# A four-sublayer hybrid trunk in split float32: the order of its first microseconds, and its first projection item in blocks of 128 tokens

## The chip, the core and the metric

The kernel runs on one core of one Trainium2 chip, as one launch. The metric is the device time in microseconds (us), median of three runs. Engines are called as in the profile: PE is the matrix engine (PEld its weight loads), DVE the vector engine, ACT the scalar engine, POOL the GpSimd engine, SP the engine that only issues loads and stores.

## The reference

The input `x` is one sequence of 512 tokens with 1024 features, in float32. It passes two layers. Each has a token mixer and a gated feed-forward block with a short causal convolution, and after each of these four sublayers stands `x = LayerNorm(alpha * x + f(x))`. Layer 0 mixes by gated linear attention, layer 1 by a gated delta rule. The change lies in the very first step, the input projection of layer 0:

```python
def gla_mixer(x, w_in, w_gk2, b_gk, norm_w, w_out):
    proj = x @ w_in                      # (512 x 1024) @ (1024 x 3088)
    q, k, v, gate, gk_lr = jnp.split(proj, [hk, 2 * hk, 2 * hk + hv, 2 * hk + 2 * hv], axis=-1)
    gk = jax.nn.log_sigmoid((gk_lr @ w_gk2 + b_gk).astype(jnp.float32)) / GLA_NORMALIZER
    ...
```

`gk_lr` has 16 columns and `w_gk2` is the 16 x 512 low-rank factor of the decay.

## The kernel before

All activations are kept feature-major: `xh` and `xl` hold x transposed, as 8 chunks of 128 features by 512 tokens. Every float32 operand of a large product is split in two: a high part, rounded to the PE's type fp32r, and a low part, the rest (`split_out`: ACT writes the high part, DVE subtracts it from the source). A product is three products: high by high, low x by high weight, high x by low weight. `wh`/`wl` are the two parts of a weight, `raw` the weight as loaded (three buffers), `wts` holds four split weights.

An **item** is 128 output columns of a projection: a 1024 x 128 weight, 8 chunks, 24 products into one PSUM bank (`fm_mms`). The plan is a list of items; `prefetch` issues the loads and splits of the next items (`issue`), and `fm_items` runs them. The first four items (`HEADSTART`: a query head, a key head, the low-rank item, a query head) run in two halves of 256 tokens, since the tokens come in four blocks of 128: the first half of all four needs blocks 0 and 1 alone. `late` (true for the first half of the first item) puts the eight low-weight products last. The low-rank item (`issue_rep`, the "rep" item) has 16 columns, repeated to 96.

The opening (`load_x`) runs so: `h` tiles (one for a block of 128 tokens and half the features) are loaded, block 0 from the SP queue, block 1 from the ACT queue; `x_part` transposes one `h` tile on PE in four steps into a bank `xT` and splits it into `xh`, `xl`. Two constant products on the tile `reset` into a bank `warm` stand ahead of the transposes, two behind them. The weight of the first item is loaded in two halves on the SP queue behind block 0 of x, and split behind all four x parts. Blocks 2 and 3 are loaded after it, and split by the task `second`, which is run (`pump`) between products.

The order of work on an engine is the order of the program, kept by hand where it matters (`keep_in_program_order` on PE while `pin` is set; `behind`, and `opening`, which puts the splits of the first items behind the first x parts). Later tasks are set by a clock of planned costs (`clk`, `spawn`, `until`). `gla_consts` loads the low-rank factor `gk` six times over, one for each group of 16 rows, from the POOL queue, and splits it as `gk2`; its first use is the product `z` of `prepare`.

Of the kernel before, what the change touches and what calls it, by code (L numbers as in the profile page):

```python
# [15 lines left out]
P = 128  # L16
# [36 lines left out]
class Trunk:  # L53
# [3 lines left out]
    def __init__(self, ctx, tc):  # L57
        self.tc = tc
        self.nc = nc = tc.nc
        self.n = 0  # L60
        ec = ctx.enter_context
        ap = ec(tc.tile_pool(name="acts", bufs=1))
        self.xh = ap.tile([P, NC, S], F32R, name="xh", tag="xh")
        self.xl = ap.tile([P, NC, S], F32R, name="xl", tag="xl")
        self.wp = ec(tc.tile_pool(name="wts", bufs=WB))
        self.mp = ec(tc.tile_pool(name="mem", bufs=SLOTS))
        self.rp = ec(tc.tile_pool(name="raws", bufs=RAWB))
        self.cp = ec(tc.tile_pool(name="const", bufs=1))
# [10 lines left out]
        nc.gpsimd.memset(self.reset, 1.0)  # L79
        nc.gpsimd.memset(c4(self.reset)[:, :, 0:1], 0.0)  # L80
# [12 lines left out]
        self.tabled = None  # L93
        self.wide = None
        self.block = None
        self.next_block = 0.0
        self.late = []
        self.first = None


    def uid(self, s):
# [118 lines left out]
    def issue(self, item):  # L220

        nc = self.nc
        if item[0] == "rep":
            return self.issue_rep(*item[1:])
        raw = self.rp.tile([P, 1024], F32, name=self.uid("raw"), tag="raw")
        used = 1024
        if item[0] == "fm":
            _, w, col = item
            r3 = raw.rearrange("p (c f) -> p c f", c=NC)
            w3 = w[:, col:col + P].rearrange("(c p) f -> p c f", p=P)  # L230
            step = NC if self.issued else NC // 2
# [66 lines left out]
    def fm_mms(self, ps, w, lo, hi, late=False):  # L298

        o = ps[:, lo:hi]  # L300
        if not isinstance(w, list):
            for c in range(NC):
                for i, x in enumerate((self.xh, self.xl)):
                    self.mm(ps[:96, lo:hi], w[:, c, :96], x[:, c, lo:hi], c + i == 0, c + i == NC)
                if c % 2:
                    self.pump()
            return
        if late:
            for c in range(2 * NC):
                wt = w[c % NC // 4][c // NC][:, blk(c % 4)]  # L310
                self.mm(o, wt, self.xh[:, c % NC, lo:hi], c == 0, c == 2 * NC - 1)
                if c < NC:
                    self.mm(o, wt, self.xl[:, c, lo:hi], False, False)
                if c % 2:
                    self.pump()
            return
        for c in range(NC):
            xh, xl = self.xh[:, c, lo:hi], self.xl[:, c, lo:hi]
            wh, wl = (t[:, blk(c % 4)] for t in w[c // 4])
            self.mm(o, wh, xh, c == 0, False)  # L320
            self.mm(o, wh, xl, False, False)
            self.mm(o, wl, xh, False, c == NC - 1)
            if c % 2:
                self.pump()

    def fm_items(self, items):
# [112 lines left out]

    def opening(self, *parts):  # L440

        if self.issued < 4:
            for ins, other in zip(parts, self.first):
                self.behind(ins, other)

    def rsqrt(self, y, x, n):

# [35 lines left out]
    def load_x(self, x):  # L483
# [1 line left out]
        nc = self.nc  # L485
        self.h = [[self.slot("h") for _ in range(2)] for _ in range(NTB)]

        def load(eng, tb):
            for hf in range(2):
                eng.dma_start(self.h[tb][hf], x[blk(tb), blk(hf, S)])  # L490
                self.set(("h", tb, hf))

        def constant(n):
            for _ in range(n):
                self.tc.keep_in_program_order(nc.tensor.matmul(ps, self.ident, self.reset, start=True, stop=True))  # L495
# [12 lines left out]
        self.look = LOOKAHEAD  # L508
        self.prefetch()
        for tb in range(2, NTB):  # L510
            load(nc.sync, tb)

        def second():
            for tb in range(2, NTB):
                for hf in range(2):
                    self.x_part(tb, hf)
                yield 1.2

            for t, row in self.late:
# [229 lines left out]
    def gla_consts(self, w_gk2, b_gk, norm_w):  # L749
        nc = self.nc  # L750

        raw = self.slot("gk")
        for i in range(6):
            nc.gpsimd.dma_start(raw[16 * i:16 * i + 16, :], w_gk2)
        self.gk2 = self.keep([96, S], "gk2", F32R)
        nc.scalar.copy(self.gk2, raw[:96, :])
        nc.vector.tensor_sub(self.gk2[32:64, :], raw[32:64, :], self.gk2[32:64, :])
        self.gla_nw = self.keep([P, 256], "gla_nw")
        self.late.append((self.gla_nw, norm_w))

# [665 lines left out]
```

## Time and profile before

| | |
|---|---|
| median of 3 runs | 1278.29 us (1278.29 to 1278.38) |
| the profiled execution's own time | 1277.96 us |
| its span | 1276.2 us |
| PE busy | 1263.8 us, 99% of the span |
| DVE, ACT, POOL busy | 783.5, 552.8, 111.1 us |
| moved by DMA | 126.53 MB, mean 99 GB/s |

The span runs from the first to the last instruction of the profiled execution; what lies around it is 1.8 us. A row of a timeline has the start, the duration, the engine, the line and the operation, what it writes and reads, how often, and in brackets how long its engine had been idle and who ended that. The durations of products are modelled to the end of their pipeline, so two products that follow each other overlap; the time that a product costs is the distance between two starts. A product of two fp32 operands makes two rows, a product of fp32r operands one row. Shapes are partitions by elements; the profile writes both types as f32 on PE.

### The profile page before, as it was taken

What the parts mean: (1) busy time and instruction counts of PE and PEld (TensorE: products, weight loads), DVE (VectorE), ACT (ScalarE), POOL (GpSimd) and SP (SyncE); (2) the same over time, 40 slices, a digit from 0 to 9 for tenths busy, and PEclk for the clock granted to TensorE, in tenths of its full rate; (3) what the DMA queues carried; (4) which work ended last, traced back from release to release, by engine and by line L of the source; (5) the groups of instructions that cost most, each with busy time, mean ns of one, the idle gap of its engine ahead of it and who ended that gap; (6) DMA issues with size and microseconds to landing.
All of it is one profiled execution on the core that took longest, in us unless ns stands there. A gap on an engine that the chain in (4) does not pass through costs nothing.

```text
span 1276.2 us, 17247 instructions
## 1 busy us (share of the span) xinstructions
PE 1263.8 (99%) x6686; PEld 1070.0 (84%) x6686; DVE 783.5 (61%) x1381; ACT 552.8 (43%) x1050; POOL 111.1 (9%) x153
## 2 busy tenths in 40 slices
PE   9999999999999999999999999999999999999997
PEld 8878888988888888889888888988988888888886
DVE  3953466676643466555789955679577653366656
ACT  4654444634421344435765544543644431244430
POOL 4000000070000000001013120100052000000000
PEclk9999999999999999999999999999999999999999
DMA  7322224143333333351354331234053333333331
GB/s 200 116 69 66 67 85 131 50 129 103 99 99 97 93 93 98 100 151 66 101 150 114 119 77 51 68 116 134 16 151 104 93 98 99 99 99 99 94 104 66
DMA packets 167234, 126.53 MB, mean 99 GB/s; under 512 B 16104, under 2 KB 139818, under 8 KB 167152
## 3 DMA queue, kind: packets, MB, share of 16 engines
q1 hardware_dynamic: 162832, 116.28, 30.7%
q0 software_dynamic: 3888, 8.50, 2.2%
q8 instruction: 52, 0.85, 0.3%
q10 hardware_dynamic: 432, 0.66, 0.2%
q14 instruction: 30, 0.25, 0.1%
HBM read 119.63 MB, written 5.78 MB: 98 GB/s over the span
## 4 chain that ended last, share of the span: by engine, by line
PE 94%; DVE 3%; ACT 1%; issue 1%; DMA 0%; POOL 0%; DVEq 0%; ACTq 0%; POOLq 0%
PE fm L160 50%; PE tm L160 35%; PE o L160 2%; PE xT L177 1%; PE R L160 1%; PE V L160 1%; PE qkT L177 1%; PE vn L160 1%; PE pq L160 1%; PE pg L160 1%; PE yT L177 1%; DVE wl L438 1%; PE s L160 0%; PE warm L495 0%; PE qs L160 0%
## 5 line engine op out<-in xcount | busy, mean ns | idle before, releaser
L438 DVE TENSOR_TENSOR wl<-raw,wh 128x1024 fp32r<-128x1024 f32 (+1 forms) x190 | 238.7, 1258 | 314.0 <-ACT wh L438 313.8
L160 PE MATMUL fm<-xh,wh 128*128 128x512 f32 (+2 forms) x1104 | 404.3, 367 | 0.0
L160 PE MATMUL fm<-xl,wh 128*128 128x512 f32 (+2 forms) x1104 | 401.5, 365 | 0.0
L160 PE MATMUL fm<-xh,wl 128*128 128x512 f32 (+1 forms) x1088 | 397.0, 366 | 0.0
L438 ACT CAST wh<-raw 128x1024 fp32r<-128x1024 f32 (+1 forms) x190 | 198.9, 1047 | 276.6 <-PE tm L160 166.3
L160 PEld LDWEIGHTS fm<-xh,wh 128*128 128x128 f32 (+1 forms) x1104 | 207.8, 188 | 33.1 <-ACT wh L438 0.4
L160 PEld LDWEIGHTS fm<-xl,wh 128*128 128x128 f32 (+1 forms) x1104 | 207.9, 188 | 32.4
L160 PEld LDWEIGHTS fm<-xh,wl 128*128 128x128 f32 x1088 | 204.7, 189 | 33.7 <-DVE wl L438 0.2
L681 DVE SCALAR_TENSOR_TENSOR conv<-fm,ffn_cw,conv 128x511 f32<-128x511 f32 (+1 forms) x176 | 130.7, 746 | 3.0
L160 PE MATMUL tm<-wl,gh 128*128 128x512 f32 x290 | 112.4, 388 | 0.0
L160 PE MATMUL tm<-wh,gl 128*128 128x512 f32 x290 | 112.4, 388 | 0.0
L160 PE MATMUL tm<-wh,gh 128*128 128x512 f32 x290 | 112.4, 388 | 0.0
L438 ACT CAST gh<-conv 128x512 fp32r<-128x512 f32 x44 | 27.3, 621 | 125.1 <-DVE conv L696 124.9
L160 PE MATMUL tm<-wh,xh 128*128 128x512 f32 x192 | 79.6, 415 | 0.1
L160 PE MATMUL tm<-wh,xl 128*128 128x512 f32 x192 | 75.2, 392 | 0.0
L160 PE MATMUL tm<-wl,xh 128*128 128x512 f32 x192 | 75.1, 391 | 0.0
L691 ACT ACTIVATE conv<-conv 128x512 f32<-128x512 f32 x44 | 27.8, 632 | 95.1 <-DVE conv L681 95.0
L160 PEld LDWEIGHTS tm<-wh,gl 128*128 128x128 f32 x290 | 54.5, 188 | 11.2
L160 PEld LDWEIGHTS tm<-wl,gh 128*128 128x128 f32 x290 | 54.5, 188 | 11.2
L160 PEld LDWEIGHTS tm<-wh,gh 128*128 128x128 f32 x290 | 54.5, 188 | 11.1
L679 ACT ACTIVATE conv<-fm,ffn_cw 128x512 f32<-128x512 f32 x88 | 60.0, 681 | 0.2
L982 DVE SCALAR_TENSOR_TENSOR conv<-fm,gdn_cw,conv 128x509 f32<-128x509 f32 (+2 forms) x72 | 53.3, 744 | 4.1 <-ACT conv L980 3.5
(279 smaller groups left out, 1536.0 us busy)
## 6 DMA issues: line engine op xcount, KB each, us to landing
raw<-in_ffn_w_in_dram SPq DMA_DIRECT2D x88, 512.0 KB, 3.7
raw<-in_ffn_w_out_dram SPq DMA_DIRECT2D x44, 512.0 KB, 3.7
raw<-in_gdn_w_in_dram SPq DMA_DIRECT2D x32, 512.0 KB, 4.1
raw<-in_gla_w_in_dram SPq DMA_DIRECT2D x23, 512.0 KB, 3.5
raw<-in_gla_w_out_dram SPq DMA_DIRECT2D x8, 512.0 KB, 3.6
raw<-in_gdn_w_out_dram SPq DMA_DIRECT2D x8, 512.0 KB, 3.7
hd<-h POOLq DMA_DIRECT2D x8, 256.0 KB, 2.5
dt<-drow POOLq DMA_DIRECT2D x8, 256.0 KB, 5.1
```

Source lines behind the costliest of these rows:

```text
L160: t = self.nc.tensor.matmul(out, a, b, start=start, stop=stop)
L177: t = self.nc.tensor.transpose(out, a, self.ident[:n, :n])
L438: return self.nc.scalar.copy(dst_h, src), self.nc.vector.tensor_sub(dst_l, src, dst_h)
L679: nc.scalar.activation(a, ps, AF.Identity, scale=tap(2))
L681: nc.vector.scalar_tensor_tensor(a[:, d:], ps[:, :S - d], tap(2 - d), a[:, d:], ALU.mult, ALU.add)
L691: nc.scalar.activation(a, a, AF.Gelu)
L982: self.conv = nc.vector.scalar_tensor_tensor(a[:, d:], ps[:, :S - d], tap(3 - d), a[:, d:], ALU.mult, ALU.add)
```

## The change

Seven edits, all in the opening:

1. The tile `reset` is set by DVE, not by POOL, and the constant products use it alone; the second pair of them is gone.
2. All four `h` tiles of blocks 0 and 1 are loaded from the SP queue. The two halves of the first weight go to the ACT queue, ahead of everything on it. The loads of the second and third item follow block 1 on the SP queue, then blocks 2 and 3.
3. The splits are chained in the order in which they are needed: x part (0,0), first half of the first weight, x part (0,1), second half.
4. The first item runs by `first_mms`: block 0 with 24 products of 128 tokens, then the transposes of block 1 (`between`), then block 1 with 24 products of 128 tokens.
5. The second item has its low-weight products last (`late`, now for item 1).
6. The low-rank factor is loaded by a task (`factor`): a POOL copy that reads the last x low part of block 1 stands ahead of the six loads, and the split of `gk2` is put behind the last x part.
7. In `opening`, each split is put behind the one before it, rather than all behind the last x part.

```diff
-        nc.gpsimd.memset(self.reset, 1.0)
-        nc.gpsimd.memset(c4(self.reset)[:, :, 0:1], 0.0)
+        nc.vector.memset(self.reset, 1.0)
+        nc.vector.memset(c4(self.reset)[:, :, 0:1], 0.0)
...
-                nc.sync.dma_start(r3[:, c:c + step, :], w3[:, c:c + step, :])
+                (nc.sync if self.issued else nc.scalar).dma_start(r3[:, c:c + step, :], w3[:, c:c + step, :])
...
-        for n in (S, used) if self.issued == 0 else (used,):
-            cols = slice(0 if n < used or self.issued else S, n)
-            self.opening(*self.split_out(wh[:, cols], wl[:, cols], raw[:, cols]))
+        pieces = [blk(j, S) for j in range(used // S)] if self.issued == 0 else [slice(0, used)]
...
+    def first_mms(self, ps, w):
+
+        def terms(tb, i):
+            for x in (self.xh, self.xl):
+                for c in range(4 * i, 4 * i + 4):
+                    self.mm(ps[:, blk(tb)], w[i][0][:, blk(c % 4)], x[:, c, blk(tb)], c == 0 and x is self.xh, False)
+
+        def low(tb, i):
+            for c in range(4 * i, 4 * i + 4):
+                self.mm(ps[:, blk(tb)], w[i][1][:, blk(c % 4)], self.xh[:, c, blk(tb)], False, c == NC - 1)
+
+        for tb in range(2):
+            for i in range(2):
+                terms(tb, i)
+                low(tb, i)
+            if tb == 0:
+                self.between()
+        self.pump()
...
-                self.fm_mms(banks[i], ws[i], half * 256, half * 256 + 256, self.pin and not half and i == 0)
+                if self.between and not half and i == 0:
+                    self.first_mms(banks[i], ws[i])
+                    self.between = None
+                else:
+                    self.fm_mms(banks[i], ws[i], half * 256, half * 256 + 256, self.pin and not half and i == 1)
...
-        load(nc.sync, 0)
-        load(nc.scalar, 1)
+        for tb in range(2):
+            for hf in range(2):
+                load(tb, hf)
+        self.prefetch()
...
-        constant(2)
-        for hf in range(2):
-            for tb in range(2):
-                self.first = self.x_part(tb, hf)
-        constant(2)
+        self.opening(*self.x_part(0, 0))
+        self.opening(*self.pieces[0]())
+        self.opening(*self.x_part(0, 1))
+        self.opening(*self.pieces[1]())
...
+        def factor():
+            raw = self.slot("gk")
+
+            nc.gpsimd.tensor_copy(raw[:, :1], self.xl[:, NC - 1, 255:256].bitcast(F32))
+            for i in range(6):
+                nc.gpsimd.dma_start(raw[16 * i:16 * i + 16, :], w_gk2)
+            yield 8.0
+            yield from self.until(("x", NTB - 1))
+            self.behind(nc.scalar.copy(self.gk2, raw[:96, :]), self.last[0])
+            self.behind(nc.vector.tensor_sub(self.gk2[32:64, :], raw[32:64, :], self.gk2[32:64, :]), self.last[1])
```

What PE runs first, before the change (`xT_112`, `xT_126` are the two halves of block 0, `xT_119`, `xT_133` those of block 1; `fm_198` is the bank of the first item; behind the rows shown come fourteen more of its products by `wh_145`):

```order
L495 MATMUL warm_109<-reset_88,ident_80 128x512 x2
L177 MATMUL xT_112<-ident_80,h_96 128x128 x4
L177 MATMUL xT_119<-ident_80,h_98 128x128 x4
L177 MATMUL xT_126<-ident_80,h_97 128x128 x4
L177 MATMUL xT_133<-ident_80,h_99 128x128 x4
L495 MATMUL warm_109<-reset_88,ident_80 128x512 x2
L160 MATMUL fm_198<-xh,wh_145 128x256
L160 MATMUL fm_198<-xl,wh_145 128x256
```

And after it, as far as the first products of the second item (`xT_117`, `xT_126` block 0; `xT_183`, `xT_190` block 1; `fm_158` the first item, `fm_250` the second):

```order
L536 MATMUL warm_114<-reset_88 128x512 x2
L178 MATMUL xT_117<-ident_80,h_96 128x128 x4
L178 MATMUL xT_126<-ident_80,h_97 128x128 x4
L161 MATMUL fm_158<-xh,wh_111 128x128 x4
L161 MATMUL fm_158<-xl,wh_111 128x128 x4
L161 MATMUL fm_158<-xh,wl_112 128x128 x4
...
L178 MATMUL xT_183<-ident_80,h_98 128x128 x4
L178 MATMUL xT_190<-ident_80,h_99 128x128 x4
L161 MATMUL fm_158<-xh,wh_111 128x128 x4
...
L161 MATMUL fm_250<-xh,wh_199 128x256
```

The 24 products of 256 tokens have become 48 of 128, and the transposes of block 1 stand between the two sets.

ACT before, at the same place (`wh_145` first item, `wh_153` second):

```order
L490 DMA h_98<-in_x_dram 128x512
L490 DMA h_99<-in_x_dram 128x512
...
L438 CAST xh<-xT_112 128x4x128
L438 CAST xh<-xT_119 128x4x128
L438 CAST xh<-xT_126 128x4x128
L438 CAST xh<-xT_133 128x4x128
L438 CAST wh_145<-raw_142 128x512 x2
L438 CAST wh_153<-raw_151 128x1024
```

ACT after (`wh_111` first item, `wh_199` second):

```order
L234 DMA raw_108<-in_gla_w_in_dram 128x4x128 x2
...
L469 CAST xh<-xT_117 128x4x128
L469 CAST wh_111<-raw_108 128x512
L469 CAST xh<-xT_126 128x4x128
L469 CAST wh_111<-raw_108 128x512
L469 CAST xh<-xT_183 128x4x128
L469 CAST xh<-xT_190 128x4x128
L469 CAST wh_199<-raw_197 128x1024
```

The two halves of the weight are split among the x parts of block 0, and block 1 comes after them; DVE's subtractions follow in the same order.

More of the change, by code (lines that the diff above doesn't have):

```diff
@@ L258, in issue @@
         wl = self.wp.tile([P, 1024], F32R, name=self.uid("wl"), tag="wl")
-        for n in (S, used) if self.issued == 0 else (used,):
-            cols = slice(0 if n < used or self.issued else S, n)
-            self.opening(*self.split_out(wh[:, cols], wl[:, cols], raw[:, cols]))
+        pieces = [blk(j, S) for j in range(used // S)] if self.issued == 0 else [slice(0, used)]
+        split = lambda cols: self.split_out(wh[:, cols], wl[:, cols], raw[:, cols])
+        if self.issued == 0:
+            self.pieces = [lambda cols=cols: split(cols) for cols in pieces]
+        elif self.issued < 4:
+            self.opening(*split(pieces[0]))
+        else:
+            split(pieces[0])
         self.vec(1.24)
@@ L308, in fm_mms @@
         if late:
[L309 to L313, printed above, removed]
+            for c in range(NC):
+                for x in (self.xh, self.xl):
+                    self.mm(o, w[c // 4][0][:, blk(c % 4)], x[:, c, lo:hi], c == 0 and x is self.xh, False)
                 if c % 2:
+                    self.pump()
+            for c in range(NC):
+                self.mm(o, w[c // 4][1][:, blk(c % 4)], self.xh[:, c, lo:hi], False, c == NC - 1)
+                if c % 4 == 3:
                     self.pump()
@@ L324, in fm_mms @@
                 self.pump()
+    def first_mms(self, ps, w):
+        def terms(tb, i):
+            for x in (self.xh, self.xl):
+                for c in range(4 * i, 4 * i + 4):
[9 more added lines that the diff above has]
+                self.between()
+        self.pump()
     def fm_items(self, items):
@@ L336, in fm_items @@
                     banks.append(self.psum("fm"))
-                self.fm_mms(banks[i], ws[i], half * 256, half * 256 + 256, self.pin and not half and i == 0)
+                if self.between and not half and i == 0:
+                    self.first_mms(banks[i], ws[i])
+                    self.between = None
+                else:
+                    self.fm_mms(banks[i], ws[i], half * 256, half * 256 + 256, self.pin and not half and i == 1)
                 if half:
@@ L440, in opening @@
     def opening(self, *parts):
-        if self.issued < 4:
+        if self.first is not None:
             for ins, other in zip(parts, self.first):
                 self.behind(ins, other)
+        self.first = parts
     def rsqrt(self, y, x, n):
@@ L486, in load_x, with load, between @@
         self.h = [[self.slot("h") for _ in range(2)] for _ in range(NTB)]
-        def load(eng, tb):
+        def load(tb, hf):
+            nc.sync.dma_start(self.h[tb][hf], x[blk(tb), blk(hf, S)])
+            self.set(("h", tb, hf))
+        for tb in range(2):
             for hf in range(2):
[L490 to L495, printed above, removed]
-        load(nc.sync, 0)
-        load(nc.scalar, 1)
+                load(tb, hf)
+        self.prefetch()
+        self.look = 0
         self.tc.keep_in_program_order(nc.scalar.copy(self.warm, self.one))
         ps = self.psum("warm")
-        constant(2)
-        for hf in range(2):
-            for tb in range(2):
-                self.first = self.x_part(tb, hf)
-        constant(2)
[L508 to L511, printed above, removed]
+        for _ in range(2):
+            self.tc.keep_in_program_order(
+                nc.tensor.matmul(ps, self.reset[:, :P], self.reset, start=True, stop=True))
+        self.opening(*self.x_part(0, 0))
+        self.opening(*self.pieces[0]())
+        self.opening(*self.x_part(0, 1))
+        self.opening(*self.pieces[1]())
+        self.set(("x", 1))
+        def between():
+            for hf in range(2):
+                self.opening(*self.x_part(1, hf))
+            self.look = 1
+            self.prefetch()
+            for tb in range(2, NTB):
+                for hf in range(2):
+                    load(tb, hf)
+            self.look = LOOKAHEAD
+        self.between = between
         def second():
@@ L515, in second @@
                 for hf in range(2):
-                    self.x_part(tb, hf)
+                    self.last = self.x_part(tb, hf)
                 yield 1.2
@@ L750, in gla_consts @@
         nc = self.nc
-        raw = self.slot("gk")
-        for i in range(6):
-            nc.gpsimd.dma_start(raw[16 * i:16 * i + 16, :], w_gk2)
         self.gk2 = self.keep([96, S], "gk2", F32R)
-        nc.scalar.copy(self.gk2, raw[:96, :])
-        nc.vector.tensor_sub(self.gk2[32:64, :], raw[32:64, :], self.gk2[32:64, :])
+        def factor():
[7 more added lines that the diff above has]
+            self.behind(nc.vector.tensor_sub(self.gk2[32:64, :], raw[32:64, :], self.gk2[32:64, :]), self.last[1])
+        self.spawn(factor(), 3.0)
         self.gla_nw = self.keep([P, 256], "gla_nw")
```

## The prediction

> **What bounds the kernel now.** I read the page's busy times first, then PE's waits, then the timeline of the first 14 us engine by engine, since the change moves instructions there and nearly nowhere else.
>
> ```profile
> PE 1263.8 (99%) x6686; PEld 1070.0 (84%) x6686; DVE 783.5 (61%) x1381; ACT 552.8 (43%) x1050; POOL 111.1 (9%) x153
> PE warm L495 <- POOL reset L80: 2.0, 1, 2.0
> PE xT L177 <- DVE ln_mv L557: 0.9, 1, 0.9
> PE kt L177 <- DVE sc L872: 0.8, 1, 0.8
> PE bat L177 <- DVE ba L1017: 0.4, 1, 0.4
> ```
>
> PE is busy 99% of the span, and its listed waits outside the start come to 2.1 us. So the end moves by as much as PE's stream moves. One anchor is enough: the start of the second item, at 12.97 us. From there on PE has the same products as before, in the same order but for a few steps. The rows of PE and its weight loads as far as that anchor:
>
> ```profile
> 2.00 3.78 PE L495 MATMUL warm<-reset,ident 128*128 128x512 f32 x4 [2.00 <-POOL reset L80]
> 5.58 2.98 PE L177 MATMUL xT<-ident,h 128*128 128x128 f32 x16
> 8.39 1.88 PE L495 MATMUL warm<-reset,ident 128*128 128x512 f32 x4
> 9.80 0.59 PE L160 MATMUL fm<-xh,wh 128*128 128x256 f32 x1
> ...
> 12.01 1.12 PE L160 MATMUL fm<-xh,wl 128*128 128x256 f32 x8
> 12.97 0.28 PE L160 MATMUL fm<-xh,wh 128*128 128x256 f32 x1
> 4.96 0.18 PEld L177 LDWEIGHTS xT<-ident,h 128*128 128x128 f32 x1 [0.76 <-DMA h<-in_x_dram]
> 9.79 0.19 PEld L160 LDWEIGHTS fm<-xh,wh 128*128 128x128 f32 x1 [0.35 <-ACT wh L438]
> 13.41 0.19 PEld L160 LDWEIGHTS fm<-xh,wl 128*128 128x128 f32 x1 [0.24 <-DVE wl L438]
> ```
>
> The constant products fill time only. The first h tile is there at 4.96, the transposes run from 5.58, and the first product waits for ACT's split of the weight until 9.79. From there a product of 256 tokens takes (12.97 - 12.01) / 8 = 0.12 us, the 24 of the first item about 3 us. The engines in front of it:
>
> ```profile
> 6.67 0.59 ACT L438 CAST xh<-xT 128x512 fp32r<-128x512 f32 x1 [3.45 <-PE xT L177]
> 9.11 1.15 ACT L438 CAST wh<-raw 128x512 fp32r<-128x512 f32 x2
> 7.29 0.69 DVE L438 TENSOR_TENSOR xl<-xT,xh 128x512 fp32r<-128x512 f32 x1 [7.29 <-ACT xh L438]
> 9.98 1.28 DVE L438 TENSOR_TENSOR wl<-raw,wh 128x512 fp32r<-128x512 f32 x2
> 1.01 0.53 POOL L79 MEMSET reset<- 128x512 f32 x1
> 1.84 0.11 POOL L80 MEMSET reset<- 128x4 f32 x1
> h<-in_x_dram ACTq DMA_DIRECT2D x2, 256.0 KB, 4.7
> raw<-in_gla_w_in_dram SPq DMA_DIRECT2D x2, 256.0 KB, 6.8
> 8.11 0.38 SPq L270 DMA_DIRECT2D raw<-in_gla_w_in_dram x1
> ```
>
> **Part 1: how much sooner the first product starts.** `reset` on DVE: no row shows a DVE memset, so POOL's pair is the nearest, 0.53 + 0.11, from 0.81 (when the engines' first rows start) to 1.45 instead of 2.00. It can cost between nothing and that. The constant products take 5.58 - 2.00 = 3.58 us, so the transposes start at 5.03 instead of 5.58, and not before the h tile at 4.96: -0.55, with ends 0 and -0.62. The second pair of constant products goes; it covered the wait for the weight split and costs nothing when gone. ACT's first x split comes 6.67 - 5.58 = 1.09 behind the first transpose: from 6.12 to 6.71, where before four x splits came ahead of the weight.
>
> The first weight half now leads the ACT queue, issued about 0.81. The two rows of landing bound it: 4.7 for an h tile on that queue, 6.8 for a weight half behind block 0 of x on the SP queue, so it lands between 5.5 and 7.6. (Before, the SP row at 8.11 is released by that half.) I take about 6.7, near the middle: then ACT is free just in time, and splits it to 7.34 (0.63 of the 1.15 for two). At 7.6 all that follows is 0.9 later, at 5.5 nothing changes. So the first product starts at 7.37 instead of 9.80: -2.4 us. The second half of block 0 and of the weight follow on ACT to 7.93 and 8.55, and on DVE four subtractions of 0.68 from 6.73 end at 9.5.
>
> **Part 2: what 48 narrow products cost.** No row shows an fp32r product of 128 tokens. The nearest of the same shape are products of 128 by 128 by 128 in the second mixer, those of the same type are the 0.12 above, and transposes have the same width:
>
> ```profile
> 719.21 1.95 PE L160 MATMUL pq<-conv,conv 128*128 128x128 f32 x16
> 720.91 0.48 PE L160 MATMUL fm<-xh,wh 128*128 128x512 f32 x1
> 17.89 0.91 PEld L177 LDWEIGHTS xT<-ident,h 128*128 128x128 f32 x8
> 18.01 1.03 PE L177 MATMUL xT<-ident,h 128*128 128x128 f32 x8
> 18.64 1.07 ACT L438 CAST xh<-xT 128x512 fp32r<-128x512 f32 x2 [0.98 <-PE xT L177]
> ```
>
> The 16 rows of `pq` are eight products and take 720.91 - 719.21 = 1.70 us: 0.2125 a product, 0.106 a row. A weight load of 128 columns is never closer to the next than about 0.11 (0.91 / 8 for transposes). So a narrow product costs between half of 0.12, if only its tokens count, and 0.2125, if the saving of the fp32r type is lost at this width. I take 0.2125: it is the only real product of this shape in the trace, and every fp32r product of this kernel is at least 256 wide, so nothing shows that the type keeps its rate below. A half-rate clock in the opening gives the same price by another way (rival 3).
>
> Then block 0 takes 24 x 0.2125 = 5.1, from 7.37 to 12.47; its operands are all there by 9.5, ahead of use. The transposes of block 1 (0.91 for eight) run to 13.38. They were hidden before, in the wait for the weight; now they stand on the path. ACT starts 0.63 behind the first (18.01 to 18.64) and needs 0.59: PE goes on at 13.7 instead of 13.38. Block 1 takes 5.1 more: the second item starts at 18.8. Its split, behind the x parts on ACT, ends by 15.9 and is hidden.
>
> So the anchor moves by 18.8 - 12.97 = +5.8.
>
> **Part 3: the rest.** The second item's low parts last: the wait of 0.24 at 13.41 goes, since the low weight is used 16 products later; nothing else is late there. Blocks 2 and 3 and the rep item are loaded as early as before, and their transposes come at the anchor + 3.8 or later (16 + 8 products by 0.12 and 0.115), so no new wait. The third item's raw buffer comes free with the first item's last subtraction, now 9.5 rather than 11.26.
>
> ```profile
> 1.88 3.08 POOL L754 DMA_DIRECT2D gk<-in_gla_w_gk_dram  x6
> gk<-in_gla_w_gk_dram POOLq DMA_DIRECT2D x6, 32.0 KB, 5.6
> 12.00 0.62 ACT L756 CAST gk<-gk 96x512 fp32r<-96x512 f32 x1
> 33.44 0.40 PE L160 MATMUL fm<-xh,wh 128*128 128x512 f32 x1
> 34.83 0.40 PE L160 MATMUL z<-lr,gk 96*128 96x512 f32 x1
> ```
>
> The factor: POOL's copy waits for block 1's last low part (about 15.1), then six issues of 0.51 and 5.6 to land give 23.3 at the earliest use. ACT then waits for it ahead of the fifth item's split, which PE needs at 33.44 + 5.6, and `z` at 34.83 + 5.6: 14 us of cover. Queued behind the copy on POOL are only norm weights and column rows, whose loads waited for a later x part anyway. If the cover were gone it would cost its two splits, 0.62 and about 0.68 on DVE. Six `tm` products that change places some 90 us in wait for nothing in PE's list: 0.
>
> **The sum**: +5.8 - 0.24 = +5.6. Against the profiled execution's own 1277.96 (span 1276.2, 1.8 around it) that is 1283.6; the median lies 0.33 above that execution, so **1283.9 us**.
>
> **Rivals.**
>
> *One weight load a product (0.114).* For it speaks that 0.11 is the least distance of 128-column loads and that each fp32r product is one row. Then DVE sets part of the pace: block 0 ends at 10.1, transposes 11.0, ACT's split of block 1 at 11.33, its low part at 12.04, block 1 at 14.3. Anchor +1.35, less 0.24: +1.1, or **1279.4**; 1280.3 with the weight at 7.6. The gain of 2.4 at the front is paid back by 2.5 of products and 1.2 of transposes and split.
>
> *Only the tokens count (0.06): not slower.* Then products hide behind DVE. Block 0 ends with the last subtraction, at 9.73; transposes 10.64; the low part of block 1 at 11.65; block 1 ends at 12.8: -0.17 - 0.24 = -0.4, or **1277.9**. It decides when a narrow product falls under about 0.08. For more than 0.2% the anchor would have to be at 10.6, and DVE's six subtractions of 0.69 from 6.7, with a transpose and a split between, do not end by then; so faster by 0.2% has almost no room.
> The Trainium skill, "TensorE: Matmul & The Clock Gate", section "Back-to-back issue gap", gives N / 2.4 + 2.5 ns for one product and about 81 ns in a stream with weight loads at N = 128; by 0.081 I estimate 1278.4. At N = 256 its formula gives 109 ns, where the trace has 120, and no run here shows its 128 for this type.
>
> *The clock stays low.* Before, four rows of constant products take 3.78 us at 2.00 and 1.88 at 8.39: PE starts at half rate and is at full rate after unbroken work from 2.00 to 8.39 at most. The change leaves gaps between the transposes and among the first products. If the rate rises only 5.7 us after 7.37, the first rival loses half of that: 1279.4 + 2.9 = **1282.3**; with all 48 at half rate about 1285.8. Against it: the gaps are under 1 us each.
> The same page, section "Part 1: The HAM clock gate (the "warmup" mystery)", says that about 3.4 us of activity raise the clock and an idle window of that length lowers it; by that rule, an estimate, this rival would cost at most 1.7 us, and the transposes before agree with the rise (0.91 for eight later, 2.98 for 16 early).
>
> **Chances.** Forecast 0.50, one weight load a product 0.30, only the tokens 0.08, the clock 0.12. Below 0.2% (2.6 us, about what a measurement of this kernel tells from no change) lie rival 1, most of rival 2 and a little of the clock's: slower 0.60, same 0.37, faster 0.03. The range goes from under the first rival to the forecast with a late weight (+0.9) and some of the clock: 1278.6 to 1286.0. It leaves out most of rival 2, and a forecast that also starts at half rate, together about 0.12. The forecast's own range is 1283.0 to 1285.5.
>
> **What would show it.** Right: first item's products 0.21 apart; second item at 18 to 20 us; no 0.24 wait behind it; `gk` split near 24 with no wait of PE. Wrong: products 0.11 or less apart, a first product later than 8.5 us, or a new wait of PE behind the anchor.

## The result: 1280.03 us, and the profile after

The changed kernel takes **1280.03 us** (median of 22 runs, 1279.53 to 1280.32) against 1278.27 for the kernel before in the same session (22 runs, 1277.74 to 1278.59): a ratio of **1.0014, 95% interval [1.0008, 1.0020]**, 1.76 us more. The profiled execution has 1280.23 us and a span of 1278.5, which is 2.27 us over the profiled execution of before.

First PE's waits after (engine, what waits, for what, total in us, times, longest):

```profile
PE warm L536 <- DVE reset L80: 1.7, 1, 1.7
PE xT L178 <- DVE ln_mv L599: 1.2, 1, 1.2
PE kt L178 <- DVE sc L922: 0.7, 1, 0.7
PE cols L178 <- DMA rows<-in_gdn_conv_w_dram: 0.5, 1, 0.5
PE bat L178 <- DVE ba L1067: 0.4, 1, 0.4
PE fm L161 <- ACT wh L469: 0.3, 1, 0.3
PE fm L161 <- ACT xh L469: 0.2, 1, 0.2
```

Three rows are new: the two `fm` waits of the opening, and `cols`, a wait far behind it. Now PE's timeline of the opening:

```profile
5.23 1.91 PE L178 MATMUL xT<-ident,h 128*128 128x128 f32 x8
7.48 0.73 PE L161 MATMUL fm<-xh,wh 128*128 128x128 f32 x4 [0.34 <-ACT wh L469]
8.05 0.61 PE L161 MATMUL fm<-xl,wh 128*128 128x128 f32 x4
8.49 0.61 PE L161 MATMUL fm<-xh,wl 128*128 128x128 f32 x4
...
10.28 1.06 PE L178 MATMUL xT<-ident,h 128*128 128x128 f32 x8
11.58 0.66 PE L161 MATMUL fm<-xh,wh 128*128 128x128 f32 x4 [0.24 <-ACT xh L469]
12.31 0.66 PE L161 MATMUL fm<-xl,wh 128*128 128x128 f32 x4
...
14.15 0.61 PE L161 MATMUL fm<-xh,wl 128*128 128x128 f32 x4
14.60 0.33 PE L161 MATMUL fm<-xh,wh 128*128 128x256 f32 x1
```

A row of four products starts 0.447 us behind the one before it ((8.49 - 8.05) and its like): 0.112 us a product, not 0.2125. Block 0 runs from 7.48 to 10.28, block 1 from 11.58 to 14.60, and the second item starts at 14.60, where it started at 12.97 before: +1.63. ACT, in front of it:

```profile
6.33 0.59 ACT L469 CAST xh<-xT 128x512 fp32r<-128x512 f32 x1 [2.98 <-PE xT L178]
6.81 0.62 ACT L469 CAST wh<-raw 128x512 fp32r<-128x512 f32 x1
7.33 0.59 ACT L469 CAST xh<-xT 128x512 fp32r<-128x512 f32 x1
...
10.94 1.07 ACT L469 CAST xh<-xT 128x512 fp32r<-128x512 f32 x2 [2.50 <-PE xT L178]
```

The weight's split at 6.81 follows the x split without a wait of its own, so the first weight half had landed by then.

Where the 2.27 us between the two profiled executions went: +1.63 at the second item, -0.24 for its own wait that is gone, +0.46 for `cols` at 87.46 us, and +0.33 for `ln_mv` at the second layer (1.21 against 0.88), together 2.18. The last of them is not the change's: the same changed kernel, run again, showed 1.0 there, and the kernels below show 0.6 to 1.8. The opening differs between executions too. e1 below has the same opening, and in its profile the first product starts at 6.82 and the second item at 13.87 us, since PE's eight transposes of block 0 took 1.04 us there and 1.91 here. So a few tenths between two single profiles prove little.

### The profile page after: what moved, and what is told of

The parts are those of the page before. It is cut to its first block, busy times and chain, and to the rows that moved or that the text cites. A ratio compares the mean times of both kernels' runs of the same rounds, so it can differ in the third digit from the quotient of the medians.

```text
span 1278.5 us, 17288 instructions
## 1 busy us (share of the span) xinstructions
PE 1265.1 (99%) x6706; PEld 1071.5 (84%) x6706; DVE 783.6 (61%) x1383; ACT 552.6 (43%) x1050; POOL 111.7 (9%) x152
## 4 chain that ended last, share of the span: by engine, by line
PE 91%; issue 5%; DVE 1%; DMA 1%; POOL 0%; ACT 0%; DVEq 0%; POOLq 0%; ACTq 0%
PE fm L161 48%; PE tm L161 34%; PE o L161 2%; PE xT L178 1%; PE R L161 1%; PE V L161 1%; PE qkT L178 1%; PE vn L161 1%; PE pq L161 1%; PE pg L161 1%; PE yT L178 1%; PE s L161 0%; PE qs L161 0%; PE ks L161 0%; DMA raw<-in_ffn_w_in_dram 0%
## 5 line engine op out<-in xcount | busy, mean ns | idle before, releaser
L161 PE MATMUL fm<-xh,wl 128*128 128x512 f32 (+2 forms) x1096 | 397.0, 365 | 0.0
L161 PEld LDWEIGHTS fm<-xh,wh 128*128 128x128 f32 x1112 | 208.4, 188 | 34.0 <-ACT wh L469 0.7
L161 PEld LDWEIGHTS fm<-xl,wh 128*128 128x128 f32 x1112 | 208.4, 188 | 32.5 <-DVE xl L469 0.2
```

The costliest lines, as they stand in the source:

```text
L161: t = self.nc.tensor.matmul(out, a, b, start=start, stop=stop)
```

## The experiments

Each was timed beside the kernel before, which had 1278.23 us in the runs of e1 to e4, 1278.27 in those of e5 to e8, 1278.08 in those of e9 to e12 and 1278.07 in those of e13 and e14.

### What do narrow products cost? e2, e5

e2 is the kernel before with nothing changed but the width of the first item's products:

```diff
-                self.fm_mms(banks[i], ws[i], half * 256, half * 256 + 256, self.pin and not half and i == 0)
+                if self.pin and not half and i == 0:
+                    for tb in range(2):
+                        self.fm_mms(banks[i], ws[i], tb * P, tb * P + P, True)
+                else:
+                    self.fm_mms(banks[i], ws[i], half * 256, half * 256 + 256)
```

> The kernel before with one edit: the first half of its first item runs as 48 products of 128 tokens, block by block, instead of 24 of 256. Theory A (a narrow product costs one weight load, 0.112 us): 48 x 0.112 - 24 x 0.12 = +2.5 us at the second item's start, of which 0.2 come back because the wait for the second item's low part goes: 1280.5 to 1280.8. Rival C (narrow products are only slow in the changed kernel, by its gaps; by themselves they cost half a wide one): 0, 1278.1 to 1278.3. Rival D (0.2125 a product, as predicted): +7.3, about 1285.

1280.30 us (11 runs), 2.07 over before, ratio 1.0017 [1.0008, 1.0026]. PE's timeline in e2:

```profile
8.88 0.43 PE L160 MATMUL fm<-xh,wh 128*128 128x128 f32 x1
...
10.83 1.06 PE L160 MATMUL fm<-xh,wl 128*128 128x128 f32 x8
11.72 0.28 PE L160 MATMUL fm<-xh,wh 128*128 128x128 f32 x1
...
14.40 0.33 PE L160 MATMUL fm<-xh,wh 128*128 128x256 f32 x1
```

Eight products take 11.72 - 10.83 = 0.89 us, 0.111 each. The first half of the item takes 14.40 - 8.88 = 5.52 us where 24 wide products took 12.97 - 9.80 = 3.17: 2.35 more in the traces, 2.07 in the medians. So narrowness alone makes the kernel slower by about as much as the whole change does (1.76). That 1280.30 is a little under the 1280.5 of the lower bound is not explained further; the size of the product is.

e5 goes on to 96 products of 64 tokens, to see whether 0.112 belongs to the tokens or to the product (against e2):

```diff
-                    for tb in range(2):
-                        self.fm_mms(banks[i], ws[i], tb * P, tb * P + P, True)
+                    for tb in range(4):
+                        self.fm_mms(banks[i], ws[i], tb * 64, tb * 64 + 64, True)
```

> The kernel before, with the first half of the first item as 96 products of 64 tokens instead of 24 of 256 (in the narrow kernel these were 48 of 128, 0.112 us apart, 1280.30 us). Theory A: a product costs one load of 128 weight columns, about 0.11 us, whatever its tokens: 96 x 0.112 = 10.75 us, 5.4 more than the 48 of 128, so 1285.4 to 1285.9 us. Theory C: the tokens set the distance (0.112 for 128 tokens, so 0.056 to 0.08 for 64): the 96 take 5.4 to 7.7 us, so 1280.3 to 1282.6 us.

1293.78 us (4 runs, 1293.03 to 1294.13): far over both. PE's timeline in e5 tells both parts:

```profile
9.47 0.28 PE L160 MATMUL fm<-xh,wh 128*128 128x64 f32 x1
9.58 0.28 PE L160 MATMUL fm<-xl,wh 128*128 128x64 f32 x1
...
12.93 0.36 PE L160 MATMUL fm<-xl,wh 128*128 128x64 f32 x1
13.10 0.40 PE L160 MATMUL fm<-xh,wh 128*128 128x64 f32 x1
13.32 0.40 PE L160 MATMUL fm<-xl,wh 128*128 128x64 f32 x1
```

Until 12.93 a product of 64 tokens costs 0.112 us, as one of 128 does: theory A's floor holds, and C, that tokens set the distance, is out. A floor can also be a fixed price of any product. A row of the kernel before speaks against that: 16 rows of products with 64 weight columns and 64 tokens, with the next product at 746.81 us:

```profile
745.74 1.14 PE L160 MATMUL V<-T,am 64*64 64x64 f32 x16
```

They are (746.81 - 745.74) / 16 = 0.067 us apart, and the rows of `pq`, with 128 columns, 0.106. Since 64 or 128 tokens make no difference at 128 columns, that points to the columns of the weight as the price. These products are of fp32 and fill 64 partitions, and no run varied the columns alone.

From 13.10 on a product of e5 costs 0.213 us. PE waits for nothing there; its clock fell. The stretches of e5 (from and to in us, length, PE busy and its instructions, granted clock, share of the DMA engines, GB/s):

```profile
12.00:13.00 1.00, 1.00 (x11) 0.99 1.08 348
13.00:14.00 1.00, 1.00 (x7) 0.50 1.34 223
...
28.00:32.00 4.00, 4.00 (x28) 0.74 0.00 0
```

The clock is 0.50 from 12.98 (0.02 us of the first stretch) to 30.08 (2.08 us of the last): 17.1 us. The 64-token products end at 26.33, so the fall costs 13.35 x (1 - 0.112 / 0.213) + 3.75 x (1 - 0.120 / 0.213) = 8.0 us, and theory A's 1285.4 to 1285.9 with it is 1293.4 to 1293.9, near the measured 1293.78.

### What stands between the blocks, and what would be without narrow products: e3, e4

e3 is the changed kernel with block 1 transposed and split ahead of block 0's products:

```diff
-        self.set(("x", 1))
+        for hf in range(2):
+            self.opening(*self.x_part(1, hf))
...
-            for hf in range(2):
-                self.opening(*self.x_part(1, hf))
```

> The changed kernel with the transposes and splits of block 1 ahead of the first item's products rather than between its two blocks; the later order is that of the kernel before. Theory A: the 0.87 us of transposes and the waits of 0.24 and 0.28 leave the path, but the first product now waits for the last h tile of block 1 (landed at 8.05) and its transposes: it starts at about 8.5 instead of 7.48, so the second item starts near 13.9 instead of 14.6; with the column rows' wait gone as well 1278.6 to 1278.9. Rival B (the products' width and place do not matter, the loads do): no gain at the second item, 14.6, and 1279.4.

1278.87 us (11 runs), 0.64 over before, ratio 1.0005 [0.9996, 1.0014]; theory A's numbers. In e3's timeline no transpose stands between the products of the two blocks:

```profile
8.26 0.64 PE L161 MATMUL fm<-xh,wh 128*128 128x128 f32 x4
...
10.52 0.61 PE L161 MATMUL fm<-xh,wl 128*128 128x128 f32 x4
10.96 0.61 PE L161 MATMUL fm<-xh,wh 128*128 128x128 f32 x4
...
13.64 0.33 PE L161 MATMUL fm<-xh,wh 128*128 128x256 f32 x1
```

The first product comes 0.78 later than in the changed kernel and the second item 0.96 sooner: starting block 0 ahead of block 1's transposes lost more than it gained. The `cols` wait is not in e3's list either, so some of the 1.1 us between the two kernels may be that.

e4 keeps the change's queues, `reset` and factor, but runs the first item as 24 products of 256 tokens, by halves of the features:

```diff
-        for tb in range(2):
-            for i in range(2):
-                terms(tb, i)
-                low(tb, i)
-            if tb == 0:
-                self.between()
+        for i in range(2):
+            terms(i)
+            low(i)
+            if i == 0:
+                self.between()
```

with `x_part(0, hf)`, `x_part(1, hf)` and the weight's half ahead of each other in that order.

> The changed kernel with its first item as 24 products of 256 tokens again: x parts (0,0), (1,0), first half of the weight, (0,1), (1,1), second half, and the products in the same order of need. All other edits stay. Theory A: ACT has the first half of the weight split at about 9.0 and the second at about 10.7; products as fast as before (0.12); the second item starts near 12.3, that is 0.7 sooner than before, no wait for low parts: 1277.2 to 1277.6, about 0.9 faster than the kernel before. Rival B (the loss comes from the loads' order or the low-rank factor's place): still 1279 or more.

**1277.32 us** (11 runs), 0.91 under before, ratio 0.9993 [0.9984, 1.0002]: theory A again, and the lowest median of the study, though its interval just holds 1. Its second item starts at 12.19 us, and it has no `cols` wait:

```profile
12.19 0.28 PE L161 MATMUL fm<-xh,wh 128*128 128x256 f32 x1
```

So the change's other edits, with wide products, seem good for some 0.9 us, and the narrow products, with the transposes between them and the `cols` wait, take 2.7 back (1280.03 - 1277.32). The load queues have no part in that gain: e9 below is e4 with the queues of before, and has 1277.29. What is left (`reset`, the order of the splits and products, the second item's low parts last, the later factor) no run took apart.

e8 is e4 with the `h` tiles loaded in the order of use:

```diff
-        for tb in range(2):
-            for hf in range(2):
+        for hf in range(2):
+            for tb in range(2):
                 load(tb, hf)
```

> The kernel with the first item as 24 products of 256 tokens (1277.32 us), its x tiles now loaded in the order in which they are transposed: first halves of blocks 0 and 1, then the second halves. Theory A: the wait of 0.86 us for the third tile goes, the first product starts 0.3 to 0.6 earlier: 1276.7 to 1277.0 us. Rival: all four tiles and the weight are needed before the stream is under way, and the last one lands no sooner: 1277.3 us.

1277.53 us (11 runs), no gain, as the rival has it, but by another cause. The second item started at 11.52, 0.67 sooner than in e4; PE's timeline of e8 gives it back at the fourth item, and ACT's says why:

```profile
18.15 0.39 PE L161 MATMUL fm<-xh,wl 128*128 128x256 f32 x1 [0.62 <-DVE wl L470]
15.79 1.05 ACT L470 CAST wh<-raw 128x1024 fp32r<-128x1024 f32 x1 [4.35 <-DMA raw<-in_gla_w_in_dram]
```

The load of that item's weight now ends last; ACT stood 4.35 us for it. A front earlier than e4's meets this wait: e9, whose second item starts at 11.22, waits 0.8 us at the same place.

### The wait at the column rows: e1

The prediction put six `tm` products that change places near 90 us at nothing. e1 moves the column transposes back to their old place among them:

```diff
-COLS_DELAY = 64.0
+COLS_DELAY = 65.0
```

> The changed kernel with the column tasks due one unit of the planner's clock later (COLS_DELAY 65 for 64), which puts back the place of six tm products ahead of the column transposes; nothing else moves on PE. Theory A (the change costs 1.4 us in the first stage and 0.6 us in a new wait of PE for the rows of the delta rule's convolution weights near 87 us): the wait of 0.5 us for these rows goes, the second item still starts at 14.6 us, time 0.5 to 0.6 under the changed kernel, 1279.4 to 1279.5. Rival B (that wait is an accident of one execution, or only moves elsewhere): no change, 1280.0.

1279.51 us (11 runs), 1.28 over before, ratio 1.0010 [1.0001, 1.0018], and the `cols` wait is gone from PE's list. The 0.5 us agree with the wait in the trace and with theory A; the two intervals overlap, and the changed kernel's own two medians lie 0.23 apart (1280.03, 1279.80), so the medians alone don't prove it. The second item was not at 14.6 in e1's profile but at 13.87; that is the opening's difference between executions, told above, which begins ahead of the first product (the row is e1's):

```profile
6.82 0.66 PE L161 MATMUL fm<-xh,wh 128*128 128x128 f32 x4 [0.76 <-ACT wh L469]
```

The load of the rows is issued at 84.59 us before, at 84.52 after and at 85.20 in e1. Its size and the time from issue to landing, in this order:

```profile
rows<-in_gdn_conv_w_dram POOLq DMA_DIRECT2D x1, 48.0 KB, 2.0
rows<-in_gdn_conv_w_dram POOLq DMA_DIRECT2D x1, 48.0 KB, 2.8
rows<-in_gdn_conv_w_dram POOLq DMA_DIRECT2D x1, 48.0 KB, 2.1
```

The stretches around it, first before, then after:

```profile
84.00:85.00 1.00, 1.00 (x7) 1.00 0.85 328
85.00:86.00 1.00, 1.00 (x6) 1.00 0.23 63
```

```profile
84.00:85.00 1.00, 1.00 (x6) 1.00 0.60 74
85.00:86.00 1.00, 1.00 (x6) 1.00 0.99 381
```

Before, a weight load ran at 84 to 85 and the rows came behind it in a quiet stretch (63 GB/s). After, the transposes stand at the same time but the weight loads, which follow the products, are later, and the rows travel in the fullest microsecond (381 GB/s). In e12 and e7, which have the place of the change, they land after 2.7 and 2.6 us and PE waits 0.4 and 0.3. That the sharing delays them is read from these rows; no run took the weight load away alone.

### The load queues, the factor, `reset`: e6, e7, e11

e6 gives the changed kernel the queues of before: block 1 of x on ACT's, the first weight behind block 0 on SP's.

```diff
-                (nc.sync if self.issued else nc.scalar).dma_start(r3[:, c:c + step, :], w3[:, c:c + step, :])
+                nc.sync.dma_start(r3[:, c:c + step, :], w3[:, c:c + step, :])
...
-            nc.sync.dma_start(self.h[tb][hf], x[blk(tb), blk(hf, S)])
+            (nc.scalar if tb == 1 else nc.sync).dma_start(self.h[tb][hf], x[blk(tb), blk(hf, S)])
```

> The changed kernel with the queues of before: block 1 of x on ACT's queue, the first weight behind block 0 on SP's. Theory A: the weight's place at the head of a queue is what starts the first product early; its first half now lands about 8.1 us as in the kernel before, one split of 0.6 follows, so the first product starts near 8.7 instead of 7.48 and nothing behind it makes that up: 1280.9 to 1281.3 us. Rival: the wait for the weight is covered by DVE's splits behind it: 1280.0 us, no change.

1285.26 us (6 runs, 1280.23 to 1288.21), neither theory. The profiled execution is the fastest one, with a first product at 7.91 instead of 7.48 us (ACT split the first weight half from 7.24 on, so it had landed before the expected 8.1); this one and the next had 1280.23 and 1280.69 at a granted clock of 0.998, and the one such execution of e13 had 1279.88, so the queues by themselves cost between nothing and 0.7. The other four had 1284.77 to 1288.21 at 0.995 to 0.991. That is taken up below.

e7 is the changed kernel with the factor's six loads back at the start (they stand ahead of `factor` again, without the copy):

```diff
+        raw = self.slot("gk")
+        for i in range(6):
+            nc.gpsimd.dma_start(raw[16 * i:16 * i + 16, :], w_gk2)
         def factor():
-            raw = self.slot("gk")
...
```

> The changed kernel with the six loads of the low-rank factor back at the program's start, their split where the change put it. Theory A: the factor is hidden in both places: 1280.0 us within 0.2. Rival: its loads at the start take rate from the x tiles and the first weight, which land some tenths later: 1280.3 to 1280.8 us.

1279.67 us (11 runs), 1.40 over before where the change is 1.76 over. Hidden within some tenths; whether the later load costs 0.3 or nothing is not settled, since e7's `ln_mv` wait (0.6) happened to be the shortest seen. The rival, that early loads hold up x and the weight, does not show: the first product stands at 7.48 in both.

e11 is the kernel before with the two memsets of `reset` on DVE:

```diff
-        nc.gpsimd.memset(self.reset, 1.0)
+        nc.vector.memset(self.reset, 1.0)
...
```

> The kernel before with the two memsets of `reset` on DVE, and nothing else. By the prediction's first term the transposes start 0.35 to 0.55 us sooner, the four x splits and the weight's split follow on ACT, and the first product with them: 1277.7 to 1277.9 us. Rival: the first weight half, behind two tiles on its queue, lands no sooner and its split sets the first product: 1278.3 us, no change.

1278.33 us (11 runs), ratio 1.0001 [0.9992, 1.001]: no change. PE's timeline of e11 shows that the edit alone does not do what the term said:

```profile
2.56 3.78 PE L495 MATMUL warm<-reset,ident 128*128 128x512 f32 x4 [2.56 <-POOL ident masks.py:199]
...
10.06 0.54 PE L160 MATMUL fm<-xh,wh 128*128 128x256 f32 x1
```

The constant products of before also read `ident`, which POOL now sets at 2.56 us, so they start later, not sooner. In the change they read `reset` alone. The rival's number came out, for a reason that neither theory had.

### What makes the clock fall: e9, e10, e12, e13, e14

e12 is the changed kernel again, e13 the kernel of e6 again.

> The changed kernel again, unaltered, beside the two kernels with the queues of before. If the falls of the clock come from those queues and not from the chip or the hour: granted clock 0.998 in all executions, 1280.0 us within 0.2. Otherwise some of its executions show 0.991 to 0.995 and 1283 to 1288 us.

> The queues kernel again, unaltered. If the falls of the clock belong to this kernel: part of its executions again at a granted clock of 0.991 to 0.995 and 1283 to 1288 us, the others at 0.998 and 1280.2 to 1280.7. If they belonged to that chip or hour: all at 0.998, median 1280.2 to 1280.7 us.

e12: 1279.80 us (11 runs), ratio 1.0014 [1.0005, 1.0022], every execution at 0.998 or 0.999. e13: 1285.44 us (6 runs), five of them from 1284.88 to 1286.23 at 0.992 to 0.995, one 1279.88 at 0.998. e6 and e13 ran on two chips, and beside them the kernel before, in 23 and 17 executions, had no fall. So the falls belong to the kernel, not to the chip or the hour. The profile of e13 caught one. Its timeline and its stretches:

```profile
5.23 1.66 PE L178 MATMUL xT<-ident,h 128*128 128x128 f32 x8
7.96 0.66 PE L161 MATMUL fm<-xh,wh 128*128 128x128 f32 x4 [1.07 <-ACT wh L469]
8.45 0.61 PE L161 MATMUL fm<-xl,wh 128*128 128x128 f32 x4
...
10.76 1.05 PE L161 MATMUL fm<-xh,wl 128*128 128x128 f32 x4
11.61 1.93 PE L178 MATMUL xT<-ident,h 128*128 128x128 f32 x8
```

```profile
8.00:10.00 2.00, 2.00 (x17) 0.91 1.29 244
10.00:12.00 2.00, 2.00 (x11) 0.50 1.05 346
...
20.00:24.00 4.00, 4.00 (x23) 0.59 1.13 261
24.00:28.00 4.00, 4.00 (x37) 1.00 0.02 5
```

PE stood 1.07 us ahead of the first product, the narrow products began at 0.112, and at about 9.64 us the clock fell to half for 13.6 us (to 23.28: 3.28 of the 4 us at 0.59). Four products then take 11.61 - 10.76 = 0.85 us, 0.2125 each: the very price that the prediction had put on the type.

e10 is the kernel of e6 with one constant product of 320 columns between block 0's transposes and the first product; e14 the changed kernel, its own queues, with a copy of 320 columns on ACT ahead of the first weight split; e9 is e4 with the queues of e6, by the diff shown there. First e10's edit, then e14's:

```diff
+        self.tc.keep_in_program_order(
+            nc.tensor.matmul(ps[:, :320], self.reset[:, :P], self.reset[:, :320], start=True, stop=True))
```

> The queues kernel with one constant product of 320 columns, as used at the start, between the transposes of block 0 and the first product, so that PE does not stand still there. Theory gap: granted clock 0.998 in all executions, 1280.2 to 1280.9 us. Theory density: the narrow products are as before, the clock falls in part of the executions: median 1282 to 1288 us, granted clock 0.991 to 0.995.

```diff
+        held = nc.scalar.copy(ps[:, :320], self.reset[:, :320])
+        self.behind(held, self.first[0])
+        self.first = held, self.first[1]
```

> The changed kernel with its own queues and one copy of 320 columns on ACT between the first x split and the first weight split, so that PE stands still some 0.4 us longer ahead of the first product (0.34 before), as in the queues kernel. Theory gap and narrow products together: part of the executions at a granted clock of 0.991 to 0.995, median over 1281 us. Rival, the order of the loads: all at 0.998, 1280.2 to 1280.6 us (the 0.4 us later start alone).

> The kernel with the first item as 24 products of 256 tokens (1277.32 us), with the queues of before (as in the queues kernel, whose executions ran from 1280.2 us at a granted clock of 0.998 to 1288.2 at 0.991). Theory density: the clock falls because narrow products leave PE's array idle much of their 0.112 us; with products of 256 none falls: granted clock 0.998, 1277.3 to 1278.2 us. Theory gap: it falls because PE stands still for 0.7 us ahead of the first product, which is so here too: granted clock 0.991 to 0.995 in most executions, 1281 to 1286 us.

| | first item | PE ahead of the first product | executions with a fall | median us |
|---|---|---|---|---|
| changed kernel, e12 | 128 tokens | stands 0.34 | 0 of 33 | 1280.03, 1279.80 |
| e1 | 128 | stands 0.76 | 0 of 11 | 1279.51 |
| e7 | 128 | stands 0.34 | 0 of 11 | 1279.67 |
| e14 | 128 | stands 1.11 | 3 of 11 | 1280.18 |
| e6, e13 | 128 | stands 0.71, 1.07 | 9 of 12 | 1285.26, 1285.44 |
| e10 | 128 | constant product, then 0.56 | 0 of 11 | 1280.47 |
| e2 | 128 | two constant products | 0 of 11 | 1280.30 |
| e5 | 64 | two constant products | 4 of 4 | 1293.78 |
| e9 | 256 | stands 0.37 | 0 of 11 | 1277.29 |

(A fall is a granted clock under 0.997; the seconds are those of the profiled executions.) e14 rules out the order of the loads: its queues are the change's own, and three executions fell, to 1284.54, 1284.82 and 1285.58 us. e10 takes the falls away with one product, as the gap theory has it; e5 falls without a gap, as the density theory has it. So neither alone is the cause. That both take work out of PE's time, and the fall comes when enough is out, fits these rows, but is a reading and not shown: no run varied the work by itself. e9 does not separate the two, since its gap was 0.37, not the 0.7 expected. How much is enough the runs don't say, and the gap of one profile does not order the kernels: e1 had 0.76 and fell in none of 11, e6 had 0.71 and fell in 4 of 6, e14's 1.11 stands in an execution without a fall, and e10's profile has another stand of 0.66 between the transposes.

## Why the prediction was wrong

The direction came out, the size didn't: 1283.9 forecast, 1280.03 measured, and the case that happened was the first rival, with 1279.4.

**The failed step is the narrow product at 0.2125 us in part 2.** It measured 0.112. The 48 products took 2.80 + 3.02 = 5.8 us where the sum has 10.2, and so the second item moved by 1.63 us and not by 5.8. The step had taken the `pq` rows as "the only real product of this shape" (`pg`, `vn`, `qs`, `ks` and others have it too, but none of them is of fp32r) and left the row of weight loads quoted next to it, 0.91 for eight, to the first rival. That row was the price: a product carries one load of 128 columns, and e5 bears it out, with 64 tokens at the same 0.112. (That `pq` costs 0.2125 because its products make two rows, with a load each, fits, but no run took it apart.) The Trainium skill, "TensorE: Matmul & The Clock Gate", section "LDWEIGHTS (loading the stationary operand)", puts a load at its columns / 1.2 ns, an estimate of 107 ns for 128, near the measured 112. For the 81 ns of the Trainium skill's section "Back-to-back issue gap" on the same page, by which the prediction worked out 1278.4, the narrow products here have 112, and the measurement decides.

**Part 1 held.** First product at 7.48 (forecast 7.37); ACT did not wait for the first item's weight. That the two agree within 0.11 is in part luck, since the same opening started at 6.82 in e1's profile. The weight's place at the head of a queue has a small share at most: with the queues of before (e6) the first product comes at 7.91, still 1.9 sooner than the 9.80 of before. The term for `reset` could not be tested by itself (e11).

**The blocks' seam held.** Transposes, split and wait took 11.58 - 10.28 = 1.30 us (forecast 1.23), and e3 gives the seam back. By the measured price alone the forecast's second item would start at 18.8 - 4.8 = 14.0; the other 0.6 to 14.60 lies mostly in the heads of the two blocks, 0.57 and 0.73 us for the first four products instead of 0.45 (8.05 - 7.48, 12.31 - 11.58).

**Part 3 held but for one line.** The 0.24 wait is not among PE's waits any more. The factor's split came at 21.86 with PE waiting for nothing, sooner than 24 because the anchor was. "Six `tm` products ... 0" was wrong: with their move the rows land 2.8 us after their issue instead of 2.0, and PE waits 0.46 us for them in the trace; e1 gives some 0.5 back.

**The rivals.** The first one's 14.3 for the second item was 0.3 short, and its 1279.4 lacks the `cols` wait. The second, tokens only, is out by e5. The third, the clock, shows in no granted clock of the 33 executions of the changed kernel, but the prediction's ground against it, "the gaps are under 1 us each", does not hold: e6, with a gap of 0.71 in its profile, fell in 4 of 6. By the Trainium skill, "TensorE: Matmul & The Clock Gate", section "Why this matters for your kernels", one should leave no idle gaps of over about 3 us between bursts; e13 kept to that, with a longest stand of 1.07, and fell. The lengths of the falls, 13.6 and 17.1 us, agree with four and five of the 3.413 us windows that the Trainium skill gives in the same page's section "Part 1: The HAM clock gate (the "warmup" mystery)".

## What to carry to other kernels

Before splitting a product into narrower ones, price it by the row of weight loads: below the width at which the tokens take as long as the load (here between 128 and 256, 0.112 against 0.120 us), each further halving doubles the cost of the whole and gains only an earlier start. Ask of an earlier start what else comes in front of the next item; here the edits other than the width were worth some 0.9 us, and only with wide products, and an earlier front than that met a wait for the fourth item's weight. Narrow products (of 128 tokens behind a stand of PE, or of 64 without one) halved its clock for 14 and 17 us in the two profiles that caught it, in some executions and not in others, so look at the clock of every execution and not only at the profiled one.

## What the runs showed of the hardware

- An fp32r product with a 128-column weight costs 0.112 us with 64 or 128 tokens and 0.120 with 256; at half clock 0.213 with 64, 128 and, in e5's second item, about 0.21 with 256 tokens.
- The clock falls under a PE that the profile calls busy all the time (e5: busy 1.00 at 0.50), and it came in lengths of 13.6 and 17.1 us, one profile each.
- The same opening took 1.91 us for its eight first transposes in one execution and 1.04 in another (the changed kernel, e1), and its first product started at 7.48 and 6.82 us.
- DVE sets the 128x512 `reset` in 0.48 us, against 0.53 on POOL:

```profile
0.99 0.48 DVE L79 MEMSET reset<- 128x512 f32 x1 [0.99 <-PEq L1462]
```
